# Twelve of 22 feed-forward tiles by seven products, additions on another ring, and moved clears, multiplies and a table load in the mixers

## The chip, the cores and the metric

One NeuronCore of one Trainium2 chip. The metric is the device time of one execution in microseconds, the median over several executions; lower is better. TensorE (PE in the rows) multiplies, VectorE (DVE), ScalarE (ACT) and GpSimd (POOL) work on its results, SyncE (SP) issues the transfers. Each engine takes its own instructions in order.

## What is computed

Two layers over 512 tokens of width 1024, in float32. A layer is a half-weighted feed-forward network, a mixer, and a second such network; an RMS norm stands before each, and one at the end. The first layer's mixer ("even") joins a compressed, selected and windowed attention (8 heads) with a dilated one (8 heads); the second's is a latent attention with 16 heads.

```python
for l in range(DEPTH):
    x = x + 0.5 * _swiglu(_rms_norm(x, ffn1_norm[l]), ffn1_w_gate[l], ffn1_w_up[l], ffn1_w_down[l])
    h = _rms_norm(x, mix_norm[l])
    x = x + (_even_mixer(h, ...) if l % 2 == 0 else _mla_mixer(h, ...))
    x = x + 0.5 * _swiglu(_rms_norm(x, ffn2_norm[l]), ffn2_w_gate[l], ffn2_w_up[l], ffn2_w_down[l])
return _rms_norm(x, final_norm)

def _swiglu(x, w_gate, w_up, w_down):
    return (jax.nn.silu(x @ w_gate) * (x @ w_up)) @ w_down
```

## The kernel before

x stays on the chip, transposed: eight tiles x0 to x7 of 128 features by 512 tokens. Seven stages follow one another: feed-forward f0, the even mixer, f1, f2, the latent mixer, f3, the final norm. Every product is made of three matmuls (`mm3`, L206 to L210): each operand is split in a high and a low part, and high·high, low·high and high·low are added in PSUM. A weight chunk is split when it has arrived: ScalarE copies the high part (wh, L160), VectorE subtracts for the low part (wl, L161).

**Feed-forward** (`ffn`, from L340). The hidden width 2816 is 22 tiles of 128, worked in two halves of 11. A tile is the gate and the up projection, silu of the one times the other, and a split (fah, fal). In the plain way ("nine") these are 48 matmuls of 512 columns, from two weight chunks. The tiles listed in `SEVEN` (L32) are computed by `seven` (L296): gate and up weights form a 2 by 2 block matrix, and x's features and tokens another, and seven block products (A11, S2, S1, S3, A12, S4, A22), each of 12 matmuls with 256 columns, take the place of eight; VectorE forms the weight sums S1 to S4 (s1 to s4, L174), splits seven blocks (L181) and combines the products (fv, fm, fn, fg, L325 to L334). After the 11 tiles of a half come the down products (L377 to L388): 8 blocks of 33 matmuls of 512 columns, each block evicted by a multiply into a temporary t and an addition into x[m]. The temporary is from the ring `t` (`self.tmp`, 4 buffers).

**Norm** (`norm`, `rms`, `squares`, `rstd`, `spread`, L212 to L275). x is split into xh (ScalarE, L217) and xl (VectorE, L218). ScalarE squares each x[k] into a buffer of the ring `t`, the first into `of` (L229); POOL adds six of them to `of` (L231); PE sums over the partitions (L241); POOL raises to the power −1/2 (rcol, L251); PE transposes it and ScalarE copies it out (rrow, L260, L261). The projections run with x unscaled; rrow and rcol come in at the evictions.

**Mixers.** A plan written by hand (`EVEN`, `MLA`) lists the units (projections, V, scores, outputs). In the even mixer, `cmp_probs` makes the compressed branch's probabilities: exp on ScalarE (L721), POOL's multiply with the mask (L722), VectorE's sum, POOL's multiply with the reciprocal (L729), PE's transposes (L732). `values` (L483) projects V into banks of the ring pa.

The order on each engine is set by the scheduler of the language, from a time line that it estimates; rings of buffers and banks (w, wh, wl three deep; fg and fa two; fn, fv, fm, s1 to s4 one; PSUM pa and pb two, pt three, pc one) bound how far it can run ahead.

Of the kernel before, what the change touches and what calls it, by code (L numbers as in the profile page):

```python
# [3 lines left out]
P = 128  # L4
D, SEQ, FF = 1024, 512, 2816
KT, NF, HF = D // P, FF // P, FF // P // 2
# [18 lines left out]
def raw(ap):  # L25
    return ap.bitcast(F32)
# [4 lines left out]

SEVEN = (4, 6, 8, 10, 12, 14, 16, 18, 20)  # L32

# [44 lines left out]
class Core:  # L78
# [185 lines left out]
    def rms(self, tiles, eng=None):  # L264
        col = self.rstd(self.squares(tiles, eng), D)
        return col, self.spread(col, self.keep.tile([P, SEQ], F32, name="rrow", bufs=2))

    def norm(self, gi):
        xs = [self.split(self.x[k], self.g[:, gi * 8 + k:gi * 8 + k + 1], "x", 8) for k in range(KT)]
        if gi == 0:  # L270
            with self.tc.issue_after(self.last.ins):
                col, row = self.rms(self.x, self.nc.vector)
        else:
            col, row = self.rms(self.x)
        return xs, col, row  # L275
# [64 lines left out]
    def ffn(self, name, l, gi, then=None):  # L340

        nc = self.nc
        with self.tc.tile_pool(name="ff", bufs=1, reuse_waits="tile") as sb:
# [3 lines left out]
            for half in range(2):  # L347
# [30 lines left out]
                for m in range(KT):  # L378
                    p = self.bank(("pc", "pt")[m % 2])
                    for i in range(HF):  # L380
                        if blk % 8 == 0:
                            cur = self.chunk(name + "_d", l, half, blk // 8)
                        c = slice(blk % 8 * P, blk % 8 * P + P)
                        self.mm3(p, cur[0][:, c], cur[1][:, c], ah[i], al[i], start=i == 0, stop=i == HF - 1)
                        blk += 1
                    t = self.tmp()
                    nc.vector.tensor_tensor(t, p, R, OP.mult)
                    nc.vector.scalar_tensor_tensor(self.x[m], t, 0.5, self.x[m], OP.mult, OP.add)  # L388
# [80 lines left out]
    def pt_tiles(self, sb):  # L469
        t = [sb.tile([P, 11, P], F32R, name=f"pt{c}") for c in "hl"]  # L470
        for x in t:
            self.nc.vector.memset(raw(x[:, 0, :]), 0.0)
        return t
# [8 lines left out]

    def values(self, sb, parts, xs, scale=None, more=None):  # L483

# [5 lines left out]
        for k0 in range(0, 4, m):  # L490
            bank = self.bank("pa")
            for kt in range(k0, k0 + m):
# [41 lines left out]
    def even(self, gi):  # L534
        nc, a, kp = self.nc, self.a, self.keep
        with self.tc.tile_pool(name="ev", bufs=1, reuse_waits="tile") as sb:
            xs, rc, R = self.norm(gi)
            CR = sb.tile([P, SEQ], F32, name="CR")
            SR = sb.tile([P, SEQ], F32, name="SR")
# [118 lines left out]
            def compress(i):  # L658
# [8 lines left out]
                e = sb.tile([P, 2, 32], F32, name="e", bufs=2)  # L667
                nc.vector.memset(z, 0.0)
                nc.vector.tensor_copy(z[:, :, 0:31], hid[:, :62].rearrange("p (a b) -> p a b", b=31))
# [9 lines left out]
                for g in range(2):  # L679
                    hr = sb.tile([P, 4, 32], F32, name="hr")  # L680
                    nc.vector.tensor_copy(hr, z[:, g:g + 1, :].to_broadcast([P, 4, 32]))
                    vg = vp[:, 64 * g:64 * g + 64]
                    nc.tensor.matmul(vg, hr, w2[:, 1, 0:64], start=True, stop=True)
                    vc = C["v", g] = sb.tile([P, 4, P], F32R, name=f"vc{g}")
                    nc.vector.memset(raw(vc), 0.0)
                    for j in range(4):
                        s = slice(32 * j, 32 * j + 32)
                        nc.scalar.activation(vc[s, j, 0:64], vg[s], AF.Copy)
                        nc.vector.tensor_tensor(vc[s, j, 64:128], vg[s], raw(vc[s, j, 0:64]), OP.subtract)

            def gate(kt, p):

                gt = C["g"][:, kt, :]
                nc.vector.tensor_scalar(gt, p, rc[:, kt:kt + 1], None, OP.mult)
                nc.scalar.activation(gt, gt, AF.Exp, scale=-1.0)
                nc.vector.tensor_scalar(gt, gt, 1.0, None, OP.add)
                nc.vector.reciprocal(gt, gt)

            def nsa_vals():
# [4 lines left out]
            def cmp_probs(g):  # L704
# [10 lines left out]
                def sp(x):  # L715
                    return x.rearrange("p (a b) -> p a b", b=4).unsqueeze(3).to_broadcast([P, 4, 4, 32])
# [4 lines left out]
                nc.scalar.activation(t, t, AF.Exp, scale=-1.0)  # L721
                nc.gpsimd.tensor_tensor(t, t, mcmp[:, 1].unsqueeze(2).to_broadcast([P, 4, 4, 32]), OP.mult)  # L722
                nc.vector.tensor_reduce(st[:, 1], t, AX.X, OP.add)
# [4 lines left out]
                                        C["g"][:, :, 12 * g:12 * g + 12:3], OP.mult)  # L728
                nc.gpsimd.tensor_tensor(t, t, sp(st[:, 2]), OP.mult)  # L729
                pt = self.bank("pt")  # L730
# [21 lines left out]
    def mla(self, gi):  # L752
        nc, a, kp = self.nc, self.a, self.keep
        with self.tc.tile_pool(name="ml", bufs=1, reuse_waits="tile") as sb:
            xs, rc, R = self.norm(gi)


# [57 lines left out]
            def vals(g):  # L815
                vk = slice(512 + g % 2 * 256, 768 + g % 2 * 256)
                kv = W["kv"]
                vs[g] = self.values(sb, lambda k: (kv[0][:, vk], kv[1][:, vk]), [cn[2]])

# [218 lines left out]
```

## Time and profile before

| | |
|---|---|
| median of 3 runs | 1947.82 us (1947.81 to 1949.94) |
| profiled execution, its own time | 1949.46 us |
| its span in the trace | 1947.70 us |
| mean granted clock of TensorE | 0.988 |
| f0, even mixer, f1, f2 | 0 to 365, to 667, to 1027, to 1381 us |
| latent mixer, f3, final norm | to 1575, to 1928, to 1948 us |

The profile is one execution. Its trace holds for every instruction when it started and ended, on which engine, from which line, and what released it. Busy shares are averages over the seven stages; a stretch with PE busy for its whole length is bounded there, and in the others the list of PE's waits tells who was late. The granted clock is that of TensorE, 1.00 for 2.4 GHz and 0.5 for 1.2 GHz.

### The profile page before, as it was taken

To read this page: it belongs to the slowest core of one execution; us is meant where nothing else is said; L and a number is where in the kernel's file an instruction comes from. 1 tells how busy PE (TensorE), PEld (TensorE's weight loads), DVE (VectorE), ACT (ScalarE), POOL (GpSimd) and SP (SyncE) were. 2 spreads that over 40 slices of the span, in tenths; PEclk is the share of its full clock that TensorE was granted. 3 is DMA by queue.
4 is the path that set the end of the run, shared out by engine and by line. 5 is a ranking of instruction groups with operands and counts; after the bars stand their busy time and mean duration, and the time that the engine had idled before them with its cause. 6 is when DMAs were issued, how large, how long until landed. Compare 5 with 4: busy or idle time off the path is not lost.

```text
span 1947.7 us, 26837 instructions
## 1 busy us (share of the span) xinstructions
PE 1906.6 (98%) x10418; PEld 1653.7 (85%) x10418; DVE 1276.3 (66%) x2272; ACT 875.3 (45%) x1511; POOL 272.8 (14%) x287
## 2 busy tenths in 40 slices
PE   9999999899999999999999999999899999999997
PEld 6888998778897788888888988998788878888986
DVE  8664665468888877456656664674489786646653
ACT  7432443346576654224435432442378664324421
POOL 0000000264444400000002000000256220000001
PEclk9999999899999999999999999999999999999998
DMA  4233233322111133333332332332310123333231
GB/s 172 90 109 98 87 98 108 115 81 87 55 55 34 41 100 98 98 98 97 109 98 87 98 109 87 98 119 89 122 33 23 58 83 102 104 100 96 91 107 52
DMA packets 49839, 174.59 MB, mean 90 GB/s; under 512 B 5792, under 2 KB 6048, under 8 KB 49712
## 3 DMA queue, kind: packets, MB, share of 16 engines
q1 hardware_dynamic: 48960, 171.74, 28.1%
q8 instruction: 81, 1.33, 0.3%
q10 hardware_dynamic: 720, 1.08, 0.1%
q14 instruction: 46, 0.38, 0.1%
q0 software_dynamic: 32, 0.07, 0.0%
HBM read 170.76 MB, written 2.10 MB: 89 GB/s over the span
## 4 chain that ended last, share of the span: by engine, by line
PE 71%; issue 19%; DVE 4%; ACT 3%; POOL 2%; DMA 0%; POOLq 0%; ACTq 0%; DVEq 0%
PE pa L208 8%; PE pa L209 8%; PE pa L210 8%; PE pb L209 5%; PE pb L210 5%; PE pb L208 5%; PE pt L208 5%; PE pt L209 5%; PE pt L210 5%; PE pc L210 3%; PE pc L208 3%; PE pc L209 3%; PE pc L435 2%; PE pt L424 2%; PE pb L603 1%
## 5 line engine op out<-in xcount | busy, mean ns | idle before, releaser
L161 DVE TENSOR_TENSOR wl<-w,wh 128x1024 fp32r<-128x1024 f32 x241 | 305.2, 1267 | 247.9 <-ACT wh L160 247.4
L160 ACT ACTIVATE wh<-w 128x1024 fp32r<-128x1024 f32 x241 | 254.6, 1057 | 459.9 <-PE pt L209 188.6
L208 PE MATMUL pa<-xh,wh 128*128 128x512 f32 (+1 forms) x784 | 294.4, 376 | 5.8 <-ACT wh L160 2.3
L209 PE MATMUL pa<-xl,wh 128*128 128x512 f32 (+1 forms) x784 | 292.5, 373 | 0.0
L210 PE MATMUL pa<-xh,wl 128*128 128x512 f32 (+1 forms) x784 | 292.2, 373 | 0.0
L231 POOL TENSOR_TENSOR of<-of,t 128x512 f32<-128x512 f32 x36 | 56.0, 1554 | 1375.1 <-issue 1005.6
L209 PE MATMUL pb<-xl,wh 128*128 128x512 f32 (+1 forms) x704 | 244.2, 347 | 0.2
L208 PE MATMUL pb<-xh,wh 128*128 128x512 f32 (+1 forms) x704 | 243.9, 346 | 0.1
L210 PE MATMUL pb<-xh,wl 128*128 128x512 f32 (+1 forms) x704 | 243.5, 346 | 0.0
L208 PEld LDWEIGHTS pa<-xh,wh 128*128 128x128 f32 x784 | 148.8, 190 | 33.8 <-ACT wh L160 3.7
L210 PEld LDWEIGHTS pa<-xh,wl 128*128 128x128 f32 x784 | 148.8, 190 | 26.3 <-DVE wl L161 0.8
L209 PEld LDWEIGHTS pa<-xl,wh 128*128 128x128 f32 x784 | 149.2, 190 | 24.2 <-DVE xl L218 0.2
L209 PEld LDWEIGHTS pb<-xl,wh 128*128 128x128 f32 x704 | 133.4, 189 | 18.6 <-DVE xl L218 2.6
L208 PEld LDWEIGHTS pb<-xh,wh 128*128 128x128 f32 x704 | 133.4, 189 | 16.9 <-ACT wh L160 0.5
L210 PEld LDWEIGHTS pb<-xh,wl 128*128 128x128 f32 x704 | 133.4, 189 | 16.3 <-DVE wl L161 0.4
L180 ACT ACTIVATE wh<-w 128x512 fp32r<-128x512 f32 x72 | 45.5, 632 | 210.7 <-PE pb L209 198.4
L208 PE MATMUL pc<-fah,wh 128*128 128x512 f32 x352 | 137.0, 389 | 0.0
L209 PE MATMUL pc<-fal,wh 128*128 128x512 f32 x352 | 137.0, 389 | 0.0
L210 PE MATMUL pt<-fah,wl 128*128 128x512 f32 x352 | 136.9, 389 | 0.0
L210 PE MATMUL pc<-fah,wl 128*128 128x512 f32 x352 | 136.9, 389 | 0.0
L208 PE MATMUL pt<-fah,wh 128*128 128x512 f32 x352 | 136.9, 389 | 0.0
L209 PE MATMUL pt<-fal,wh 128*128 128x512 f32 x352 | 136.9, 389 | 0.0
(255 smaller groups left out, 4115.4 us busy)
## 6 DMA issues: line engine op xcount, KB each, us to landing
w<-f_g SPq DMA_DIRECT2D x88, 512.0 KB, 3.5
w<-f_u SPq DMA_DIRECT2D x88, 512.0 KB, 3.5
w<-f_d SPq DMA_DIRECT2D x88, 512.0 KB, 3.5
w<-ev_in SPq DMA_DIRECT2D x16, 512.0 KB, 3.5
w<-ev_out SPq DMA_DIRECT2D x8, 512.0 KB, 3.3
w<-mla_out SPq DMA_DIRECT2D x8, 512.0 KB, 3.2
x<-x SPq DMA_DIRECT2D x8, 256.0 KB, 5.1
w<-ev_vb SPq DMA_DIRECT2D x4, 512.0 KB, 3.3
```

The source lines that it names most:

```text
L160: nc.scalar.activation(h[:, :cols], w[:, :cols], AF.Copy)
L161: nc.vector.tensor_tensor(l[:, :cols], w[:, :cols], raw(h[:, :cols]), OP.subtract)
L180: nc.scalar.activation(h[:, c], src, AF.Copy)
L208: nc.tensor.matmul(out, wh, xh, start=start, stop=False)
L209: nc.tensor.matmul(out, wh, xl, start=False, stop=False)
L210: nc.tensor.matmul(out, wl, xh, start=False, stop=stop)
L231: eng.tensor_tensor(parts[0], parts[0], sq, OP.add)
L424: nc.tensor.transpose(ps[:, i * P:(i + 1) * P], pt[:, c:c + P], self.ident)
L435: nc.tensor.matmul(ps[:, q0:], v(kt), PT[j][:, b, :], start=start and kt == 0 and j == 0, stop=stop and kt == 3 and j == 1)
L603: nc.tensor.matmul(ps[:, :n], q[qi][:, qt * P:(qt + 1) * P], kd[ki][j][:, :n], start=j == 0, stop=j == 1)
```

## The change

Six things. (1) `SEVEN` lists twelve tiles in place of nine, and some stand beside one another: (4,5), (7,8), (13,14), (16,17), (19,20). (2) The down phase's temporary comes from the ring `fg` of the feed-forward pool, not from `t`. (3) `warm_exp`, after the norm of both mixers, computes one exp whose result nobody reads. (4) Three clears move from VectorE to POOL. (5) The first V of the latent mixer takes its banks from pb. (6) In the compressed branch the mask comes in at the gate column (four small VectorE operations) in place of POOL's multiply with the mask, and VectorE does the multiply with the reciprocal. Line numbers after the change are 5 higher from `norm` on, then up to 8.

```diff
--- before.py
+++ after.py
@@ -29,7 +29,7 @@
-SEVEN = (4, 6, 8, 10, 12, 14, 16, 18, 20)
+SEVEN = (4, 5, 7, 8, 10, 11, 13, 14, 16, 17, 19, 20)
 FFNS = {"f0": ("f1", 0, 0), "f1": ("f2", 0, 2), "f2": ("f1", 1, 3), "f3": ("f2", 1, 5)}
@@ -264,6 +264,11 @@
     def rms(self, tiles, eng=None):
         col = self.rstd(self.squares(tiles, eng), D)
         return col, self.spread(col, self.keep.tile([P, SEQ], F32, name="rrow", bufs=2))
+
+    def warm_exp(self):
+
+        e = self.keep.tile([P, 4], F32, name="rcol", bufs=16)
+        self.nc.scalar.activation(e[:, 0:1], self.x[KT - 1][:, 0:1], AF.Exp, scale=0.0)
     def norm(self, gi):
         xs = [self.split(self.x[k], self.g[:, gi * 8 + k:gi * 8 + k + 1], "x", 8) for k in range(KT)]
@@ -383,7 +388,7 @@
                         c = slice(blk % 8 * P, blk % 8 * P + P)
                         self.mm3(p, cur[0][:, c], cur[1][:, c], ah[i], al[i], start=i == 0, stop=i == HF - 1)
                         blk += 1
-                    t = self.tmp()
+                    t = sb.tile([P, SEQ], F32, name="fg", bufs=2)
                     nc.vector.tensor_tensor(t, p, R, OP.mult)
                     nc.vector.scalar_tensor_tensor(self.x[m], t, 0.5, self.x[m], OP.mult, OP.add)
             if then is not None:
@@ -469,7 +474,7 @@
     def pt_tiles(self, sb):
         t = [sb.tile([P, 11, P], F32R, name=f"pt{c}") for c in "hl"]
         for x in t:
-            self.nc.vector.memset(raw(x[:, 0, :]), 0.0)
+            self.nc.gpsimd.memset(raw(x[:, 0, :]), 0.0)
         return t
     def project(self, xs, *key):
@@ -480,7 +485,7 @@
                      start=k == 0, stop=k == KT - 1)
         return p
-    def values(self, sb, parts, xs, scale=None, more=None):
+    def values(self, sb, parts, xs, scale=None, more=None, tag="pa"):
         nc = self.nc
@@ -488,7 +493,7 @@
         v = sb.tile([P, 4, 4, P], F32R, name="v", bufs=2)
         m = SEQ // c
         for k0 in range(0, 4, m):
-            bank = self.bank("pa")
+            bank = self.bank(tag)
             for kt in range(k0, k0 + m):
                 p = bank[:, (kt - k0) * c:(kt - k0 + 1) * c]
                 t = slice(kt * P, kt * P + P)
@@ -535,6 +540,7 @@
         nc, a, kp = self.nc, self.a, self.keep
         with self.tc.tile_pool(name="ev", bufs=1, reuse_waits="tile") as sb:
             xs, rc, R = self.norm(gi)
+            self.warm_exp()
             CR = sb.tile([P, SEQ], F32, name="CR")
             SR = sb.tile([P, SEQ], F32, name="SR")
             nc.sync.dma_start(CR, a["cos_p"])
@@ -665,7 +671,7 @@
                                          start=l0 == 0, stop=l0 == 15)
                 z = sb.tile([P, 2, 32], F32, name="z", bufs=2)
                 e = sb.tile([P, 2, 32], F32, name="e", bufs=2)
-                nc.vector.memset(z, 0.0)
+                nc.gpsimd.memset(z, 0.0)
                 nc.vector.tensor_copy(z[:, :, 0:31], hid[:, :62].rearrange("p (a b) -> p a b", b=31))
                 nc.scalar.activation(e, z, AF.Exp, scale=-1.0)
                 nc.vector.tensor_scalar(e, e, 1.0, None, OP.add)
@@ -682,7 +688,7 @@
                     vg = vp[:, 64 * g:64 * g + 64]
                     nc.tensor.matmul(vg, hr, w2[:, 1, 0:64], start=True, stop=True)
                     vc = C["v", g] = sb.tile([P, 4, P], F32R, name=f"vc{g}")
-                    nc.vector.memset(raw(vc), 0.0)
+                    nc.gpsimd.memset(raw(vc), 0.0)
                     for j in range(4):
                         s = slice(32 * j, 32 * j + 32)
                         nc.scalar.activation(vc[s, j, 0:64], vg[s], AF.Copy)
@@ -695,6 +701,8 @@
                 nc.scalar.activation(gt, gt, AF.Exp, scale=-1.0)
                 nc.vector.tensor_scalar(gt, gt, 1.0, None, OP.add)
                 nc.vector.reciprocal(gt, gt)
+
+                nc.vector.tensor_scalar(gt[:, 0::3], gt[:, 0::3], mcmp[:, 1, kt, 0:1], None, OP.mult)
             def nsa_vals():
                 c = [self.chunk("ev_vsw", i) for i in range(3)]
@@ -719,14 +727,13 @@
                 nc.vector.tensor_reduce(st[:, 0], t, AX.X, OP.min)
                 nc.vector.tensor_tensor(t, t, sp(st[:, 0]), OP.subtract)
                 nc.scalar.activation(t, t, AF.Exp, scale=-1.0)
-                nc.gpsimd.tensor_tensor(t, t, mcmp[:, 1].unsqueeze(2).to_broadcast([P, 4, 4, 32]), OP.mult)
                 nc.vector.tensor_reduce(st[:, 1], t, AX.X, OP.add)
                 nc.vector.tensor_scalar(st[:, 1], st[:, 1], 1.0, None, OP.max)
                 nc.vector.reciprocal(st[:, 2], st[:, 1])
                 nc.vector.tensor_tensor(st[:, 2].rearrange("p (a b) -> p a b", b=4),
                                         st[:, 2].rearrange("p (a b) -> p a b", b=4),
                                         C["g"][:, :, 12 * g:12 * g + 12:3], OP.mult)
-                nc.gpsimd.tensor_tensor(t, t, sp(st[:, 2]), OP.mult)
+                nc.vector.tensor_tensor(t, t, sp(st[:, 2]), OP.mult)
                 pt = self.bank("pt")
                 for qt in range(4):
                     nc.tensor.transpose(pt[:, qt * P:(qt + 1) * P], t[:, qt].rearrange("p a b -> p (a b)"),
@@ -753,6 +760,7 @@
         nc, a, kp = self.nc, self.a, self.keep
         with self.tc.tile_pool(name="ml", bufs=1, reuse_waits="tile") as sb:
             xs, rc, R = self.norm(gi)
+            self.warm_exp()
             CQ = [sb.tile([P, SEQ], F32, name=f"CQ{i}") for i in range(2)]
@@ -815,7 +823,7 @@
             def vals(g):
                 vk = slice(512 + g % 2 * 256, 768 + g % 2 * 256)
                 kv = W["kv"]
-                vs[g] = self.values(sb, lambda k: (kv[0][:, vk], kv[1][:, vk]), [cn[2]])
+                vs[g] = self.values(sb, lambda k: (kv[0][:, vk], kv[1][:, vk]), [cn[2]], tag="pb" if g == 0 else "pa")
             def keys(hp):
                 p = self.bank("pa")
```

VectorE in f0's second half, the pair of tiles 13 and 14. After the change; w_1934 and w_1935 are tile 14's weights, wl_1945 its first low parts (A11 and S2), wl_1952 those of S1 and S3; fm_2014, fn_2012 and fg_2011 are tile 13's combinations.

```order
L174 TENSOR_TENSOR s4_1941<-w_1934,s2_1939 128x512
L181 TENSOR_TENSOR wl_1945<-w_1934,wh_1944 128x512
L181 TENSOR_TENSOR wl_1945<-s2_1939,wh_1944 128x512
L330 TENSOR_TENSOR fv_2013<-fm_2014,pa_2008 128x256
L181 TENSOR_TENSOR wl_1952<-s1_1938,wh_1951 128x512
L333 TENSOR_TENSOR fm_2014<-fv_2013,pt_2010 128x512
L181 TENSOR_TENSOR wl_1952<-s3_1940,wh_1951 128x512
L335 TENSOR_TENSOR fn_2012<-fm_2014,pt_2010 128x256
L338 TENSOR_TENSOR fg_2011<-fm_2014,pb_2009 128x512
L181 TENSOR_TENSOR wl_1959<-w_1934,wh_1958 128x512
L181 TENSOR_TENSOR wl_1959<-s4_1941,wh_1958 128x512
L339 TENSOR_TENSOR fg_2011<-fg_2011,rrow_179 128x512
```

Tile 14's splits stand between tile 13's combinations, the first of them ahead of all of these; before, tile 13 was a nine.

ScalarE at the end of f0's down phase, before: wh are splits of weight chunks, xh the split of x for the even mixer, t the squares of the next norm.

```order
L217 ACTIVATE xh_3181<-x6_71,g_63 128x512
L160 ACTIVATE wh_3122<-w_3120 128x1024
L160 ACTIVATE wh_3258<-w_3256 128x1024
L229 ACTIVATE t_3191<-x1_66 128x512
L229 ACTIVATE t_3194<-x2_67 128x512
L229 ACTIVATE t_3197<-x3_68 128x512
L229 ACTIVATE t_3200<-x4_69 128x512
L217 ACTIVATE xh_3185<-x7_72,g_63 128x512
L229 ACTIVATE t_3203<-x5_70 128x512
L229 ACTIVATE t_3206<-x6_71 128x512
L229 ACTIVATE t_3209<-x7_72 128x512
```

The same place after the change:

```order
L229 ACTIVATE t_3410<-x5_70 128x512
L160 ACTIVATE wh_3295<-w_3293 128x1024
L217 ACTIVATE xh_3388<-x6_71,g_63 128x512
L229 ACTIVATE t_3413<-x6_71 128x512
L160 ACTIVATE wh_3329<-w_3327 128x1024
L160 ACTIVATE wh_3467<-w_3465 128x1024
L217 ACTIVATE xh_3392<-x7_72,g_63 128x512
L229 ACTIVATE t_3416<-x7_72 128x512
L271 ACT_TABLE_LOAD
L271 ACTIVATE rcol_3438<-x7_72 128x1
```

The squares of x5 and x6 have moved between the splits; one square and the load of the table (L271) stand behind the last chunk.

POOL at the start of the even mixer, before:

```order
L231 TENSOR_TENSOR of_3189<-of_3189,t_3206 128x512
L251 TENSOR_TENSOR rcol_3220<-rv_3221,mhalf_62 128x4
L552 TENSOR_TENSOR CR_3231<-CR_3231,rrow_3224 128x512
L553 TENSOR_TENSOR SR_3232<-SR_3232,rrow_3224 128x512
L566 TENSOR_TENSOR t_3407<-t_3407,SR_3232 128x512
```

The same place after the change:

```order
L231 TENSOR_TENSOR of_3396<-of_3396,t_3413 128x512
L477 MEMSET pth_3461 128x128
L477 MEMSET ptl_3462 128x128
L674 MEMSET z_3934 128x64
L674 MEMSET z_4295 128x64
L691 MEMSET vc0_4307 128x512
L691 MEMSET vc1_4320 128x512
L251 TENSOR_TENSOR rcol_3427<-rv_3428,mhalf_62 128x4
L558 TENSOR_TENSOR CR_3440<-CR_3440,rrow_3431 128x512
```

Six clears have come between the last addition of squares and the power (L251).

## Rows read from the trace of the kernel before

**Rows 1.** Page, part 1: busy us (share of span) x instructions, whole kernel.
```profile
PE 1906.6 (98%) x10418; PEld 1653.7 (85%) x10418; DVE 1276.3 (66%) x2272; ACT 875.3 (45%) x1511; POOL 272.8 (14%) x287
```

**Rows 2.** By stretch: window, us, PE, PEld, DVE, ACT, POOL busy (x), PEclk, DMA, GB/s.
```profile
200.08:221.06 20.98, 20.98 (x134) 19.09 (x132) 15.05 (x24) 8.92 (x14) 0.00 (x0) 1.00 0.29 101
129.33:189.20 59.87, 59.87 (x267) 49.55 (x265) 27.96 (x34) 12.43 (x14) 0.00 (x0) 1.00 0.35 105
364.82:409.75 44.93, 39.43 (x213) 34.65 (x212) 20.59 (x30) 14.17 (x21) 26.75 (x18) 0.89 0.29 95
1381.17:1423.42 42.25, 37.12 (x178) 31.35 (x176) 21.60 (x36) 19.68 (x31) 14.52 (x11) 0.88 0.27 92
1927.61:1947.70 20.09, 9.13 (x49) 8.43 (x47) 4.93 (x9) 4.72 (x8) 4.81 (x4) 0.61 0.27 104
```

**Rows 3.** PE's waits: tile and line, releaser, total us, count, longest.
```profile
PE pa L208 <- DVE x L531: 5.4, 5, 3.1
PE pa L498 <- ACT t L229: 5.0, 1, 5.0
PE pt L887 <- POOL of L231: 4.5, 1, 4.5
PE pa L499 <- DVE xl L218: 2.1, 1, 2.1
PE pt L260 <- POOL rcol L251: 1.8, 1, 1.8
PE pa L208 <- DVE v L512: 1.7, 1, 1.7
PE pt L732 <- POOL t L729: 1.3, 1, 1.3
```

**Rows 4.** PE in order of time: start us, duration us, line, operation, out<-in, form.
```profile
200.08 0.28 PE L208 MATMUL pa<-xh,wh 128*128 128x256 f32 x1
210.15 0.40 PE L208 MATMUL pa<-xh,wh 128*128 128x512 f32 x1
221.06 0.28 PE L208 MATMUL pa<-xh,wh 128*128 128x256 f32 x1
```

**Rows 5.** VectorE in order of time, a seven tile of f0, same columns.
```profile
238.00 1.29 DVE L181 TENSOR_TENSOR wl<-s,wh 128x512 fp32r<-128x512 f32 x2
...
249.04 1.22 DVE L161 TENSOR_TENSOR wl<-w,wh 128x1024 fp32r<-128x1024 f32 x1
250.18 0.68 DVE L328 TENSOR_TENSOR fm<-fv,pt 128x512 f32<-128x512 f32 x1
250.90 0.42 DVE L330 TENSOR_TENSOR fn<-fm,pt 128x256 f32<-128x256 f32 x1
251.23 0.68 DVE L333 TENSOR_TENSOR fg<-fm,pb 128x512 f32<-128x512 f32 x1
```

**Rows 6.** In order of time, start of the even mixer: ScalarE, POOL, VectorE, ScalarE.
```profile
365.80 1.66 ACT L229 ACTIVATE t<-x 128x512 f32<-128x512 f32 x3
...
366.49 9.59 POOL L231 TENSOR_TENSOR of<-of,t 128x512 f32<-128x512 f32 x6 [340.04 <-ACT t L229]
...
368.27 2.31 DVE L161 TENSOR_TENSOR wl<-w,wh 128x1024 fp32r<-128x1024 f32 x1
...
423.81 1.28 ACT L410 ACT_TABLE_LOAD   x1
```

**Rows 7.** VectorE in order of time, compressed branch, first group.
```profile
500.24 2.85 DVE L580 SCALAR_TENSOR_TENSOR q<-t,q 64x512 fp32r<-64x512 f32 x2
...
505.26 0.63 DVE L531 TENSOR_TENSOR x<-pa,x 128x512 f32<-128x512 f32 x1
```

**Rows 8.** VectorE in order of time, start of the latent mixer.
```profile
1410.18 0.69 DVE L773 SCALAR_TENSOR_TENSOR cnl<-t,cnh 128x512 fp32r<-128x512 f32 x1 [0.70 <-ACT cnh L772]
```

**Rows 9.** In order of time, final norm: ScalarE, POOL.
```profile
1929.26 2.19 ACT L229 ACTIVATE t<-x 128x512 f32<-128x512 f32 x4 [6.85 <-DVE x L388]
...
1938.42 1.02 POOL L902 TENSOR_TENSOR rcol<-rv,mhalf 128x4 f32<-128x4 f32 x1 [4.45 <-DVE rv L901]
```

## The prediction

> **What bounds the kernel now.** I first read the shares of busy time: PE 98%, DVE 66%, ACT 45%, POOL 14% [rows 1]. A number near 100% over six different stages says little about one stage, so the second view is the table by stretch [rows 2]. Its first two lines are the inside of a feed-forward stage: PE is busy for the whole of 20.98 us at a granted clock of 1.00, while DVE works 15.05 us, ACT 8.92; in a down phase PE is busy for 59.87 of 59.87 us, DVE for 27.96. There only fewer or shorter matmuls shorten the time. The other three lines are the start of the even mixer, the start of the latent mixer and the final norm: PE is busy for 39.43 of 44.93, 37.12 of 42.25 and 9.13 of 20.09 us, at clocks of 0.89, 0.88 and 0.61. There PE waits, and the list of its waits says for whom [rows 3]: 4.5 us for POOL's additions of squares before the final norm; 5.0 us for a ScalarE square (t, L229) before the latent mixer's first V; 1.8 + 1.7 + 2.1 us in the start of the even mixer; up to 3.1 us at once for VectorE's L531, and 1.3 us for POOL's L729, in the mixer's compressed branch. Each of these ends has a queue behind it, so each is followed on the engine named.
>
> A time of this kernel can tell a change from none at about 0.2%, 3.9 us. The sum goes against the profiled execution (1949.46 us); the median of the runs is 1.64 us lower, which I take off at the end.
>
> **The change, part by part.**
>
> *Twelve more tiles by seven products* (three more in each of four stages). Two neighbouring tiles start 200.08 to 210.15 (seven products) and 210.15 to 221.06 (nine) [rows 4]: 10.07 and 10.91 us. That agrees with 84 matmuls of 256 columns at .120 and 48 of 512 at .227. Twelve times 0.84 is **−10.1**, if PE stays the bound. The Trainium skill's page "TensorE: Matmul & The Clock Gate", section "Wait — 56ns, not 53.3ns?", gives columns over 2.4 GHz plus about 2.5 ns; this would be 109 and 216 ns, 9.2 and 10.4 us a tile, and −14.3 as an estimate. The rows show both shapes some 10 and 5% above that, so the sum stays with −10.1.
>
> Does PE stay the bound? VectorE does far more for a seven: sixteen operations of 512 columns at .60 from start to start, and three of 256 columns at .33 (250.90 to 251.23) [rows 5], 10.6 us, against 4.1 for a nine (two of 1.14, three of .60). Before, every seven stood next to a nine: 14.7 of 20.98 us (the row has 15.05). Now there are five pairs of sevens in each stage: 21.2 us of VectorE against 20.1 of PE. Alone that would not hold, but each pair has a nine before and behind it: three tiles need 25.3 of VectorE and 31.05 of PE. What decides is whether VectorE can run ahead. From the start of the pair's first tile, PE wants the second tile's four block groups at 10.07, 12.95, 15.8 and 18.7 us; their buffers come free at 2.88, 5.76, 8.64 and 10.07 (24 matmuls a pair of blocks). The least slack is 7.2 us, with two splits and up to four weight sums at .60 in it, 3.6. The changed order has the second tile's splits ahead of the first tile's tail, as the fence of VectorE's rows shows. I cost the pairs at nothing; what covers them is that slack.
>
> *The additions' temporary from the gate ring.* It adds and removes no instruction; it frees the ring t for the squares, and the six additions of each next norm move into the down phase. Four stages gain, each by its own chain:
> - Start of the even mixer. Before, three squares at .55 each run in a row at 365.80 after the last product, and six POOL additions take 9.59 us from 366.49 [rows 6]; the sums, the column's power and the row follow. After, only x7's square is left. PE's own work in the stretch is 96 matmuls of 256 columns and 96 of 512, 33.3 us; to it come 1.4 for sums and transposes, .7 for x7's low part and .5 for the first weight split: 35.9 against 44.93, **−9.0** (−6 to −10: the rcol wait of 1.8 may stay, since six clears now stand before the power on POOL).
> - Start of the latent mixer, where V also changes its bank. Before, the V products wait 5.0 us for pa to be released by work that stands behind the squares, though their operand was ready at 1410.18 + .69 [rows 8]; the clock then is lower for about 4 us. After: 96 matmuls of 512, 21.8, and 2.5 around them, then a chain from the last projection to the first scores. It has six VectorE steps of .60 and one of 1.14 with 1 us of waits, five ScalarE copies at .55, and .85 for the first products: 9.3. PE has only 6.4 of work in it, so about 2.9 of waiting stays, with some 1.2 lost to the clock. 34.8 against 42.25: **−7.5** (−5 to −9).
> - Final norm. Four squares in a row begin at 1929.26, POOL adds behind them, and the power of the column begins only at 1938.42 [rows 9]. With six additions done during the products, x7's square (.55) and the sum's matmuls are left after the last product's eviction (1.2 for two VectorE steps), so that the power can begin near 1931.3: **−7.0** (−6 to −7.4).
> - f1 to f2 has no wait of this kind in the list: 0.
>
> What speaks against it: the first split beside POOL's additions took 2.31 us (368.27) [rows 6], the same form alone 1.22 [rows 5], so each of the 24 additions that move can cost VectorE 1.09 us. The skill's page "SBUF — State Buffer", section "Who interferes with whom", has that rule: a VectorE instruction with two SBUF inputs contends with a GpSimd one that reads SBUF. The trace agrees by these two rows. In the down phase VectorE is idle for 31.9 of 59.87 us [rows 2], which covers it; I cost it at nothing, and the loss of that cover is a rival below.
>
> *Exp table early.* The load of 1.28 us stood on ScalarE at 423.81 before the first softmax [rows 6]; it moves under the products: **−1.3** (0 to −2.7, with the clock).
>
> *The compressed branch.* POOL's mask multiply goes, and its other multiply moves to VectorE. The wait of 3.1 us was for VectorE's L531, which began at 505.26, after two slow q operations (2.85 us for two) [rows 7] and a split. Before, the transposes' wait and the lower clock behind it cost 3.1 + 1.5; after, they wait for one VectorE multiply, about 1 us, with .4 for the clock: **−3.2** (0 to −4.6). The second group's wait for POOL's L729, 1.3: **−1.5** with the clock (0 to −2.4). The four small operations on the gate columns run when the gates are made, before any of this: 0, and 2.4 us at most at .60 each.
>
> *Clears to POOL.* On VectorE they lay beside products, 0; on POOL, ahead of the power, they may keep the 1.8 us wait, which is in the even start's bound.
>
> Sum: 10.1 + 9.0 + 7.5 + 7.0 + 1.3 + 3.2 + 1.5 = 39.6. From 1949.46 that is 1909.9, and 1.64 lower at the median: **1908 us**. All the ends together give 1902 and 1921 (46.2 and 27.1 removed); both at once are unlikely, and the forecast's own range is 1901 to 1915.
>
> **Rivals.**
> - *The mixers give half back.* A removed wait shows the next late thing. Of the 29.5 us outside the tiles 14.8 come back: 1947.8 − 10.1 − 14.8 = 1923. For it: the chains in the mixers pass through three engines, and the even start has three different releasers [rows 3]. Against it: two of the ends (even start, final norm) are bounded by PE's own matmuls. 0.20.
> - *Pairs bound by VectorE.* 21.2 − 20.14 = 1.06 for each of 20 pairs, 21.2: 1929. For it: VectorE's longer sum. Against it: 5.8 us of spare time in three tiles. 0.05.
> - *Squares slow the down phase's splits.* 24 × 1.09 = 26.2 on PE's path: 1934. For it: the 2.31 us row. Against it: 31.9 us of idle VectorE in 59.87. 0.03.
> - *Slower: the second seven of a pair waits at the first one's end.* fn, fg, fa, fal and A22's low part have single or double buffers; if the second tile's first split stood behind them, PE would wait for 2.1 us of VectorE, one ScalarE copy (.55) and one more split (.60): 3.3 us in each of 20 pairs, 66 us: 1974. It decides from (39.6 + 3.9) / 20 = 2.2 us a pair on. For it: VectorE's queue is in order and an operation waiting for PE's last product blocks what follows. Against it: the changed order puts splits ahead. 0.03.
> - *No effect.* The squares could still be placed after the last block. The changed order of ScalarE shows them among the blocks. 0.01.
>
> **How the numbers follow.** Forecast 0.68. The range 1899 to 1924 takes in its bounds and the first rival, 0.88 in all less the forecast's own misses. Faster by over 0.2%: all but the last two, 0.95; the same 0.02, for no effect and mixtures; slower 0.03.
>
> **What would show it.** A stretch of seven, seven, nine in f0's second half should last 31.05 us with PE busy throughout; a stall in it, with VectorE or ScalarE as releaser before a product of A11 or S2, makes the pair rivals true. The even start should last about 36 us, the latent one 35, the final norm 13, with POOL's additions spread over the down phases. The 5.0 and 4.5 us waits should be gone. If the stretches outside the feed-forward stages shorten by under 20 us, the first rival holds; a down phase above 60 us would show the additions in VectorE's way.

## The result, and the profile after

The changed kernel takes 1913.88 us (median of 4 runs, 1913.83 to 1914.83), the kernel before 1948.68 (4 runs, 1947.81 to 1949.94): 0.9822 of it, with a 95% interval of 0.9805 to 0.9839. The forecast was 1908, with a range of 1899 to 1924. The profiled execution took 1913.86 us, its span is 1911.7.

The page's shares, to be held against [rows 1]:

```profile
PE 1883.0 (98%) x10850; PEld 1657.4 (87%) x10850; DVE 1354.5 (71%) x2438; ACT 903.4 (47%) x1585; POOL 274.6 (14%) x291
```

PE is busy for 23.6 us less, the span is 36.0 us shorter; VectorE rose from 66% to 71%. The table by stretch, whose columns are those of [rows 2]: three tiles (13, 14 and 15: seven, seven, nine) of f0's second half, f0's second down phase, the start of the even mixer, the start of the latent mixer, the final norm.

```profile
209.32:240.38 31.06, 31.06 (x217) 29.17 (x216) 25.98 (x43) 14.54 (x24) 0.00 (x0) 1.00 0.34 102
302.50:362.34 59.84, 59.84 (x265) 49.57 (x264) 29.88 (x34) 20.48 (x26) 8.82 (x6) 1.00 0.30 92
362.34:397.84 35.50, 35.50 (x213) 31.73 (x212) 17.73 (x24) 12.47 (x17) 19.07 (x18) 1.00 0.40 129
1362.13:1396.93 34.80, 33.23 (x179) 28.11 (x177) 18.97 (x32) 17.71 (x27) 6.43 (x7) 1.00 0.35 121
1898.46:1911.72 13.26, 5.35 (x49) 5.11 (x47) 4.79 (x9) 3.05 (x5) 1.02 (x1) 0.80 0.41 158
```

The three tiles last 31.06 us with PE busy throughout (31.05 forecast). Six POOL additions (8.82 us) now lie inside the down phase, which lasts 59.84 us as before. The even start takes 35.50 in place of 44.93 us, without a wait and at full clock; the latent one, to its first scores, 34.80 in place of 42.37 (the window of [rows 2] ends just ahead of these); the final norm 13.26 in place of 20.09. POOL in order of time shows it: additions between the down phase's blocks, the clears (1.4 us in all) right after the last product, and the power at 369.74, which waits for none of them.

```profile
321.12 1.86 POOL L231 TENSOR_TENSOR of<-of,t 128x512 f32<-128x512 f32 x1 [294.70 <-ACT t L229]
328.99 1.29 POOL L231 TENSOR_TENSOR of<-of,t 128x512 f32<-128x512 f32 x1 [6.02 <-ACT t L229]
...
357.90 1.29 POOL L231 TENSOR_TENSOR of<-of,t 128x512 f32<-128x512 f32 x1 [5.50 <-ACT t L229]
362.57 0.21 POOL L477 MEMSET pth<- 128x128 f32 x1 [3.37 <-PE pt L210]
...
363.02 0.99 POOL L691 MEMSET vc<- 128x512 f32 x2
369.74 1.02 POOL L251 TENSOR_TENSOR rcol<-rv,mhalf 128x4 f32<-128x4 f32 x1 [5.73 <-DVE rv L246]
```

Of PE's waits in [rows 3] those for L229, L231, L251 and L512 are gone. The largest left within the mixers are these:

```profile
PE pb L609 <- DVE mn L412: 3.8, 4, 2.3
PE pb L209 <- DVE kl L837: 2.4, 1, 2.4
PE pb L208 <- ACT kh L836: 1.5, 1, 1.5
PE pt L739 <- DVE t L736: 1.4, 1, 1.4
```

The time by stage, from PE's first matmul of each stage in the two traces ("rest" reaches to the first matmul behind the next stage's norm; before, that is 24 and 17 us past the ends of the mixers at 667 and 1575):

| stretch | before | after | difference | forecast |
|---|---|---|---|---|
| f0, f1, f2, f3 | 1390.80 | 1380.98 | −9.8 | −10.1 |
| even start | 44.93 | 35.50 | −9.4 | −9.0 |
| even rest | 281.27 | 279.04 | −2.2 | −6.0 |
| latent start | 42.37 | 34.80 | −7.6 | −7.5 |
| latent rest | 168.24 | 168.16 | −0.1 | 0 |
| final norm | 20.09 | 13.26 | −6.8 | −7.0 |

### The profile page after: what moved, and what is told of

Its sections match the earlier page's. It is cut to its first block, busy times and chain, and to the rows that moved or that the text cites. A ratio compares the mean times of both kernels' runs of the same rounds, so it can differ in the third digit from the quotient of the medians.

```text
span 1911.7 us, 27981 instructions
## 1 busy us (share of the span) xinstructions
PE 1883.0 (98%) x10850; PEld 1657.4 (87%) x10850; DVE 1354.5 (71%) x2438; ACT 903.4 (47%) x1585; POOL 274.6 (14%) x291
## 5 line engine op out<-in xcount | busy, mean ns | idle before, releaser
L160 ACT ACTIVATE wh<-w 128x1024 fp32r<-128x1024 f32 (+1 forms) x217 | 229.2, 1057 | 357.7 <-PE pt L209 98.3
L161 DVE TENSOR_TENSOR wl<-w,wh 128x1024 fp32r<-128x1024 f32 (+1 forms) x217 | 273.0, 1259 | 159.4 <-ACT wh L160 158.3
L208 PE MATMUL pa<-xh,wh 128*128 128x512 f32 (+1 forms) x736 | 269.1, 366 | 2.8 <-ACT wh L160 2.2
L210 PE MATMUL pa<-xh,wl 128*128 128x512 f32 (+1 forms) x736 | 268.2, 364 | 0.5 <-DVE wl L161 0.5
L209 PE MATMUL pa<-xl,wh 128*128 128x512 f32 (+1 forms) x736 | 268.7, 365 | 0.0
L231 POOL TENSOR_TENSOR of<-of,t 128x512 f32<-128x512 f32 x36 | 55.9, 1552 | 1319.6 <-issue 892.5
L209 PE MATMUL pb<-xl,wh 128*128 128x256 f32 (+1 forms) x704 | 233.9, 332 | 0.2
L208 PE MATMUL pb<-xh,wh 128*128 128x256 f32 (+1 forms) x704 | 233.6, 332 | 0.0
L210 PE MATMUL pb<-xh,wl 128*128 128x256 f32 (+1 forms) x704 | 233.3, 331 | 0.0
L180 ACT ACTIVATE wh<-w 128x512 fp32r<-128x512 f32 x96 | 60.7, 632 | 237.9 <-PE pb L209 159.2
L180 ACT ACTIVATE wh<-s 128x512 fp32r<-128x512 f32 x192 | 114.9, 622 | 55.9 <-PE pa L209 26.3
```

The lines of the kernel that those rows point to most:

```text
L160: nc.scalar.activation(h[:, :cols], w[:, :cols], AF.Copy)
L161: nc.vector.tensor_tensor(l[:, :cols], w[:, :cols], raw(h[:, :cols]), OP.subtract)
L180: nc.scalar.activation(h[:, c], src, AF.Copy)
L208: nc.tensor.matmul(out, wh, xh, start=start, stop=False)
L209: nc.tensor.matmul(out, wh, xl, start=False, stop=False)
L210: nc.tensor.matmul(out, wl, xh, start=False, stop=stop)
```

## The experiments

**One part undone each.** First the ring:

```diff
-                    t = sb.tile([P, SEQ], F32, name="fg", bufs=2)
+                    t = self.tmp()
```

> The changed kernel with the down phase's temporary back in the ring t; all else as changed. Theory (the ring carries the gain of all three edges): the even start goes from 35.5 us back to about 44, the final norm from 13.3 to about 20, the latent start loses 3 to 8 us; in all 19 to 24 us more than the changed kernel, about 1935. Rival (the bank, the clears and the table load carried the two mixer starts, the ring only the final norm): 7 us more, about 1921. The feed-forward tiles stay at 20.15 us a pair in both.

1935.12 us, 21 us more. The same three stretches by window (to the first scores in the latent one; the even start here reaches 403.90):

```profile
362.37:403.90 41.53, 38.26 (x213) 33.52 (x212) 17.07 (x24) 15.55 (x23) 27.92 (x24) 0.92 0.31 101
1368.33:1412.19 43.86, 37.88 (x178) 31.73 (x177) 22.01 (x35) 21.82 (x33) 15.40 (x13) 0.89 0.27 88
1912.88:1933.00 20.12, 9.13 (x49) 8.43 (x47) 4.92 (x9) 4.72 (x8) 4.82 (x4) 0.62 0.27 104
```

The latent start is at 43.86, the final norm at 20.12, both back; the even start is at 41.5, 6.0 of its 9.4 us back, with the waits for the power (1.8) and for the first eviction of V (1.5). So the ring carries the latent start and the final norm whole, and of the even start two thirds, where the theory expected about 44 us. The first V takes its banks from pb in this run too, and the latent start is long all the same: the bank alone would not have shortened it.

Of the other 3.4 us of the even start 2.1 is the wait for xl (L218) in [rows 3], which did not come back. The traces show what took it away. Before, the six clears stood on VectorE between the last product's multiply and the addition to x7, ahead of xl:

```profile
365.02 0.69 DVE L387 TENSOR_TENSOR t<-pt,rrow 128x512 f32<-128x512 f32 x1 [3.10 <-PE pt L210]
365.68 0.17 DVE L472 MEMSET pth<- 128x128 f32 x1
...
366.19 1.02 DVE L685 MEMSET vc<- 128x512 f32 x2
367.13 1.21 DVE L388 SCALAR_TENSOR_TENSOR x<-t,x 128x512 f32<-128x512 f32 x1
...
370.50 1.75 DVE L218 SCALAR_TENSOR_TENSOR xl<-x,g,xh 128x512 fp32r<-128x512 f32 x1
```

In the run with the ring undone they are on POOL, and xl begins 3.3 us after the last product in place of 5.7:

```profile
365.67 1.16 DVE L218 SCALAR_TENSOR_TENSOR xl<-x,g,xh 128x512 fp32r<-128x512 f32 x1 [0.55 <-ACT xh L217]
```

1.4 of these 2.4 us are the clears; the rest is instructions that took longer before. No run moved the clears alone, but the new list alone (the last run below) leaves the wait at 2.1.

The bank of V, and the clears, in two runs (of the clears the first of three lines, all changed alike):

```diff
-                vs[g] = self.values(sb, lambda k: (kv[0][:, vk], kv[1][:, vk]), [cn[2]], tag="pb" if g == 0 else "pa")
+                vs[g] = self.values(sb, lambda k: (kv[0][:, vk], kv[1][:, vk]), [cn[2]], tag="pa")
...
-            self.nc.gpsimd.memset(raw(x[:, 0, :]), 0.0)
+            self.nc.vector.memset(raw(x[:, 0, :]), 0.0)
```

> The changed kernel with the latent mixer's first V back in banks of pa. Theory (what held pa were the squares behind the last products, and these now run in the down phase): 0 to 1 us more, 1914 to 1915, no wait of a V product for pa above 1 us. Rival (the bank itself was the cause): the wait of 5.0 us comes back, about 1919.

> The changed kernel with the clears back on VectorE. Theory (they lie beside products on either engine): the even start stays at 41.2 us to its first scores, the total within 1 us of 1913.9, and what differs comes from the order in the mixers. Rival (POOL's six clears ahead of the power are a cost that the forecast's bounds held, or the clears on VectorE were one): the even start moves by 1 us or more.

1913.58 and 1913.39 us. With the additions on their new ring neither part is worth a time that these runs can tell: V's wait of 5.0 us did not come back with pa (one of 1.2 us is there; the latent start is 0.7 us longer, its rest 1.1 shorter), and the even start to its first scores is 41.21 us with the clears on either engine.

The compressed branch:

```diff
-                nc.vector.tensor_scalar(gt[:, 0::3], gt[:, 0::3], mcmp[:, 1, kt, 0:1], None, OP.mult)
...
+                nc.gpsimd.tensor_tensor(t, t, mcmp[:, 1].unsqueeze(2).to_broadcast([P, 4, 4, 32]), OP.mult)
...
-                nc.vector.tensor_tensor(t, t, sp(st[:, 2]), OP.mult)
+                nc.gpsimd.tensor_tensor(t, t, sp(st[:, 2]), OP.mult)
```

> The changed kernel with the compressed branch as before: both multiplies on POOL, no mask in the gate column. Theory (as the traces of the two kernels read: only the first group gained, the second got new waits of the same size on ScalarE's and VectorE's queues): 2 to 3.5 us more, about 1916.7, with a wait of some 3 us back in the first group and the second group's losses within 0.7 us of the changed kernel's. The forecast's terms would make it 4.7 us more, 1918.6. Rival (neither group gained from this part, the order moved for other reasons): 0.

1919.38 us, 5.5 more, above both figures. 2.5 us of it lie in the even mixer's rest, within the theory's 2 to 3.5, but partly by luck. Between places up to which both kernels have done the same matmuls, the first group takes 2.8 us more, with its wait of 3.1 back. The second takes 1.1 us less, though its waits sum to 4.7 us in both, so its losses are not within 0.7 us of the changed kernel's. Another 0.4 is gained where the gates are made, and 1.2 is lost behind the wait for the second scores, which is as long as in the changed kernel: the matmuls behind it stay longer at the lower clock. What the edit itself costs there is 1.3 us. PE's waits:

```profile
PE pa L208 <- DVE x L536: 5.6, 4, 3.1
PE pt L738 <- POOL t L735: 1.3, 1, 1.3
PE pt L429 <- DVE cl L743: 0.7, 1, 0.7
```

The 0.4 is the small operation on the gate column. In the changed kernel one of the four stands on VectorE ahead of the minimum over a score tile (L412), for which PE's next scores wait, as the trace shows:

```profile
435.51 0.23 DVE L705 TENSOR_SCALAR gt<-gt,mcmp 128x8 f32<-128x8 f32 x1
435.65 0.24 DVE L700 TENSOR_SCALAR gt<-pa,rcol 128x24 f32<-128x24 f32 x1
435.80 0.28 DVE L412 CUSTOM_DVE_ANT_0 p<-pb,mdil 128x128 f32<-128x128 f32 x1
```

The other 3.1 us lie in the latent mixer (171.25 against 168.16), where nothing was edited: the scheduler, whose time line had moved, wrote another order of instructions there. That was in neither expectation, and a total alone would have charged it to this part.

The early exp, taken out of both mixers:

```diff
-            self.warm_exp()
```

> The changed kernel without warm_exp in either mixer. Theory (in the even mixer the load of 1.28 us hid a wait for POOL's rotation and VectorE's split, so taking it away gave 0.6; in the latent mixer the load has room): 0.6 to 1.2 us more, about 1914.8. The forecast's term: 1.3 more from the even mixer alone. Rival (both mixers wait for the load at the lower clock): 2.6 and more, above 1916.5.

> The changed kernel without warm_exp again, now timed more than once. Theory (0.6 us of the 2.7 us that it cost is the load in the even mixer's chain, and 0.4 in the latent mixer; the other 1.7 was a stretch at the lower clock near 600 us that falls in some executions and not in others): the fastest executions lie at 1914.5 to 1915, some at 1916.5. Rival (the lower clock there belongs to the missing early load): all executions at 1916.3 or more.

1916.62 in the first run; 1916.81, 1916.38, 1916.58 and 1914.97 later: 2.6 us more at the median. The order on PE, VectorE and POOL in the even mixer is that of the changed kernel. Of the wait before the second scores 0.6 us came back (2.93 against 2.30). Most of the rest lies 180 us later, in 10 us in which PE gets 38 matmuls done at a mean clock of 0.83 here, and 48 at 1.00 in the changed kernel; first this kernel (the run of four), then the changed one:

```profile
593.00:603.00 10.00, 7.46 (x38) 6.17 (x37) 8.11 (x17) 5.70 (x12) 0.45 (x1) 0.83 0.20 61
```

```profile
592.00:602.00 10.00, 7.46 (x48) 6.14 (x47) 9.42 (x23) 6.89 (x16) 1.00 (x2) 1.00 0.20 55
```

So the early load is worth 0.6 us at its place. Both profiled executions without it show the lower clock there, and one of the four times (1914.97) lies where 0.6 and 0.4 us alone would put it, which the rival did not allow; that this execution had no such stretch is inferred from its time. But the rival is not done with: the changed kernel and the five other profiled runs here that keep its order in the even mixer, but for the clears (the bank, the clears, fifteen tiles twice, sixteen) all have the early load, and all show 1.00 at that place. Whether the missing load brings the lower clock there, in most executions and not in all, stays open; the order and the waits ahead of that place are the same but for the 0.6 us.

**The second group.** In the changed kernel the wait for POOL's L729 is gone, but the group's waits rose from 3.7 to 4.7 us, at three other places (PE, VectorE, POOL and ScalarE, each in order of time; the first VectorE row is the first group's):

```profile
588.07 0.50 PE L208 MATMUL pa<-oh,wh 128*128 128x512 f32 x1 [1.09 <-DVE st L731]
595.32 0.51 PE L440 MATMUL pc<-pth,v 128*128 128x512 f32 x1 [1.11 <-ACT pth L432]
597.09 0.44 PE L429 MATMUL pt<-ident,p 128*128 128x128 f32 x2 [1.26 <-DVE cl L744]
```

```profile
491.41 0.69 DVE L736 TENSOR_TENSOR t<-t,st 128x512 f32<-128x512 f32 x1
...
586.09 0.69 DVE L730 TENSOR_REDUCE st<-t 128x16 f32<-128x512 f32 x1 [0.70 <-ACT t L729]
586.69 0.68 DVE L570 TENSOR_TENSOR t<-pa,CR 128x512 f32<-128x512 f32 x1
...
587.98 1.22 DVE L161 TENSOR_TENSOR wl<-w,wh 128x1024 fp32r<-128x1024 f32 x1
589.11 0.68 DVE L536 TENSOR_TENSOR x<-pa,x 128x512 f32<-128x512 f32 x1
...
590.62 1.68 DVE L736 TENSOR_TENSOR t<-t,st 128x512 f32<-128x512 f32 x1
```

```profile
590.42 1.33 POOL L573 TENSOR_TENSOR t<-t 128x512 f32<-128x512 f32 x1
```

```profile
591.78 1.29 ACT L585 ACTIVATE q<-t 64x512 fp32r<-64x512 f32 x2 [4.78 <-POOL t L573]
593.10 1.06 ACT L160 ACTIVATE wh<-w 128x1024 fp32r<-128x1024 f32 x1
594.18 0.60 ACT L743 ACTIVATE ch<-pt 128x512 fp32r<-128x512 f32 x1
594.67 1.08 ACT L432 ACTIVATE pth<-pt 128x512 fp32r<-128x512 f32 x2
```

VectorE waits for the exp at 586.09 with the reduction at the head of its queue, and a projection's rotation, a weight split and L536, which releases an output bank, stand behind it: PE waits 1.09. The multiply that was moved from POOL takes 1.68 us beside POOL's part of the rotation (L573); the first group's, with nothing on POOL, takes 0.69. The rule of the Trainium skill's page "SBUF — State Buffer", section "Who interferes with whom", that a VectorE instruction with two SBUF inputs contends with a GpSimd one that reads SBUF, agrees with these rows. The transposes then come without a wait, but their copy (L743) stands behind two copies of q and a weight split on ScalarE. A run moved that projection:

```diff
-     [... "o2 p1 q11 o3", "", ...
+     [... "o2 p1 o3", "q11", ...
```

> The changed kernel with one unit of the even mixer's plan (the projection q11) moved from beside the second group's probabilities (p1) to the next place in the list. Theory (the second group gained nothing because q11's two ScalarE copies, its weight split and its VectorE steps stand ahead of the group's copies of the transposes): the two waits of 1.3 and 1.5 us behind the transposes near 595 us shrink to under 1 us together, 1.5 to 2.5 us less, about 1912. Rival (the chain of the second group itself, from scores to transposes, ends last): nothing there changes, within 0.5 us of 1913.9.

1923.36 us, 9.5 more. At its place the theory was right in part: the wait at 588 is gone and those behind the transposes are 0.7 and 0.6, 1.3 together and not under 1, which gains 1.3 us there and not 1.5 to 2.5:

```profile
594.69 0.49 PE L440 MATMUL pc<-pth,v 128*128 128x512 f32 x1 [0.71 <-ACT pth L432]
595.81 0.44 PE L429 MATMUL pt<-ident,p 128*128 128x128 f32 x2 [0.63 <-DVE cl L744]
...
654.31 0.73 PE L208 MATMUL pa<-oh,wh 128*128 128x512 f32 x2 [2.06 <-ACT oh L622]
655.66 0.54 PE L209 MATMUL pa<-ol,wh 128*128 128x512 f32 x1 [0.62 <-POOL ol L623]
```

But the outputs at the mixer's end waited 2.1 and 0.6 for oh and ol, presumably because the projection, now late, held back the heads that use it; the even rest as a whole took 5.0 us more, and the latent mixer got another order again (172.56 against 168.16). What is gained at its place is lost again behind it.

**How many tiles by seven products.**

```diff
-SEVEN = (4, 5, 7, 8, 10, 11, 13, 14, 16, 17, 19, 20)
+SEVEN = (4, 5, 6, 8, 9, 10, 11, 12, 14, 15, 16, 18, 19, 20, 21)
```

> The changed kernel with fifteen of 22 tiles by seven products: (4,5,6), (8 to 12 across the halves), (14,15,16), (18 to 21). Theory (TensorE stays the bound, as in the pairs at 20.15 us; three sevens and a nine want 35.9 us of VectorE and 41.1 of TensorE): 12 more tiles at 0.83, 10 us less, about 1904, with runs of sevens at 10.07 us a tile. Rival (VectorE's longer work shows once three sevens follow one another): stalls within the runs, 0.5 to 3 us in each of 16, 1912 or more.

1909.88 us. The feed-forward stages gave 9.9 us, with three sevens in 30.23 us and no stall; the even rest took 1.3 us more, the latent rest 4.9. The order in the even mixer is that of the changed kernel on every engine, and so are the waits: its 1.3 us are the clock behind the wait for the second scores, where PE gets 18 matmuls done in 6 us at a mean clock of 0.57, and 22 at 0.72 in the changed kernel.

> The changed kernel with all tiles from 4 to 21 by seven products, 18 of 22. Theory: TensorE saves 24 x 0.83 = 20 us, but VectorE needs 10.6 us for each seven against 10.07; a run of eleven falls 5.8 us behind, a run of seven 3.7, against some 3.6 us by which it can run ahead, so stalls of 0 to 3 us at the end of each half: 1896 to 1904. Rival (TensorE stays the bound throughout, since VectorE begins each half far ahead): 1894. Rival (VectorE cannot run ahead in long runs, the queue's order blocks it): 0.5 us and more for each tile, 1910 or more.

1906.17 us, with tiles 4 to 21, above the theory's 1904. Six more tiles in each stage save some 1.5 us and not 5: VectorE is busy 109.5 of 115.4 us in the second half, PE waits for weight splits within the run and the down phases begin among the last products of the seven. That loses some 3.5 us a stage, of which 1.9 show as waits in f0.

```profile
187.39:302.83 115.44, 114.20 (x925) 112.63 (x924) 109.49 (x192) 58.49 (x104) 0.00 (x0) 1.00 0.32 106
```

```profile
263.07 0.38 PE L208 MATMUL pa<-xh,wh 128*128 128x256 f32 x1 [0.41 <-ACT wh L180]
```

Here VectorE is the bound, and a run of eleven reaches past what it can run ahead, as the theory had it, though the loss is larger. In the same run the second group's waits are smaller by themselves (3.6 us in place of 4.7, and 1.3 us of time), and there the scheduler put L536 and the split ahead of the waiting reduction. The run with the ring undone has that order too, and the same gain. With V back in pa, the latent mixer's order is the same whatever the list of tiles, so two more runs took that:

> The changed kernel with the fifteen tiles of the run before by seven products, and the latent mixer's first V back in banks of pa. Theory (the fifteen tiles gave their 9.9 us in the feed-forward stages; the 6.2 us that the run lost came from another order of instructions in the latent mixer, which the scheduler made, and from the clock; with V in pa the order there is that of the run with the bank undone): that run's 1913.6 less 9.9, about 1903.7, with the latent mixer's rest at 167.0 us. Rival (the loss in the mixers belongs to the longer runs of sevens, whatever the order): 1909 or more.

> As the fifteen tiles with V in pa, and one more tile by seven products (4 to 6, 8 to 15, 17 to 21). Theory (TensorE stays the bound while a nine stands within eight sevens; the stalls of the run with eighteen came from eleven in a row): 0.83 less in each of four stages, 3.3 us less than with fifteen, about 1900.4. Rival (VectorE falls behind in a run of eight that crosses the down phase, or of five at the end): 0.5 to 3 us of stalls in each stage, 1902 to 1912.

1905.43 us (1904.42 to 1907.25) and 1904.04 (1903.78 to 1904.78); of the kernel before, 0.9778 (0.9764 to 0.9793) and 0.9771 (0.9756 to 0.9785). The latent rest was 166.6 and 166.8: the loss of the run with fifteen there belonged to the order. The 1.3 us of the even rest stayed in both. The sixteenth tile gave 0.15 in f1, f2 and f3 in place of 0.83, as the rival had it: its run of five at the end lets the down phase begin among the run's last products, and there PE waits for VectorE's eviction (L392, in fg), which is half of what is missing:

```profile
314.65 0.50 PE L208 MATMUL pc<-fah,wh 128*128 128x512 f32 x1 [0.33 <-DVE fg L392]
```

Both beat the changed kernel, the one with sixteen by 9.8 us at the medians.

Last, the new list alone in the kernel before:

> The kernel before with the new list of twelve tiles alone. Theory (0.83 us for each of 12 tiles, the pairs run without a stall, the order in the mixers is that of the kernel before): 9.9 us less than the kernel before, about 1938 to 1939.6 by which of its own times one takes, pairs at 20.15 us. Rival (the pairs hold only because the additions' temporary left the ring t): stalls in the pairs or before the down phases, 1943 or more.

1943.82 us in one run, above the theory's 1939.6 and at the rival's bound. But its reason fails: pairs take 20.15 us, and the stages f1 to f3 save what they should (0.82 and 1.62 a half). The order in the mixers is that of the kernel before. What is missing is the program's start (f0 saves 1.1 in place of 2.5; the clock of its first 20 us is 0.83, 0.91 in the changed kernel), 0.8 in the even rest and 2.0 in the latent start, whose granted clock is 0.84 in place of [rows 2]'s 0.88 with the same order and the same wait of 5 us. 1.5 of these 2.0 lie ahead of that wait: seven matmuls from 1390.4 on take 0.43 us each in place of 0.23, after no wait of PE above 0.2 us in that stage. Why the clock falls there the traces do not say. The kernel before itself lay between 1947.8 and 1952.5 in these studies, the changed one between 1913.8 and 1914.8: spells at the lower clock that fall in some executions and not in others would make such a spread; these profiles suggest it, no run tested it.

## Why the prediction was right, and where it was off

The direction, the size and the range held, and the mechanism at all three edges. By its own steps:

- *Twelve more tiles* (−10.1): −9.8, pairs at 20.15, no stall. The rivals of the pairs, the slower one too, did not occur. The figure of the Trainium skill's page "TensorE: Matmul & The Clock Gate", section "Wait — 56ns, not 53.3ns?", would have made it −14.3 as an estimate; the trace does not agree, and its .120 and .227 decided. Where VectorE becomes the bound showed with eighteen tiles.
- *The ring*: the three edges gave −9.4, −7.6 and −6.8 against −9.0, −7.5 and −7.0. The run without it gave back 21 us: the latent start and the final norm whole, 6.0 of the even start, where the moved clears have a part. That the latent start met its 34.8 us so closely is in part luck: PE waited 1.6 us of it and not 2.9, and lost nothing to the clock where 1.2 was allowed, but was busy for 33.2, where the terms (21.8, 2.5 and 6.4) make 30.7. And behind the wait of 5.0 us before the change the clock was lower for some 8 us, not 4 (0.50 from 1412.2 to 1416.5, 0.59 on to 1421).
- *Additions beside the down phase's splits*: 59.84 us with six additions within. The contention shown by [rows 5, 6] costs VectorE time that it has; the rival did not occur.
- *Exp table early* (−1.3): 0.6 at its place. The step took the load for the end of the chain; behind it POOL's rotation and VectorE's split were nearly as late. After the change ScalarE's copy of q waits 0.40 us for POOL:

```profile
413.48 1.28 ACT L585 ACTIVATE q<-t 64x512 fp32r<-64x512 f32 x2 [0.40 <-POOL t L573]
```

- *The compressed branch*: the first group −2.5 against −3.2. The four operations on the gate columns were priced at 0 and cost 0.4. The second group (−1.5) is where the forecast failed: +0.5, with 1.0 more of waits, while the kernel before lost time there to the clock (0.66 from 597 to 602 us). It priced the one wait that [rows 3] names and did not follow what was late next on VectorE's and ScalarE's queues, so the first rival, a new late thing for a removed wait, held at this one place. With the exp's 0.6 these make the even rest's −2.2. Outside the tiles 26.2 of the 29.5 us came.
- *Clears and bank*: 0 each in the changed kernel, as the clears were priced. But the reading behind that price, that the clears lay beside products on VectorE, fails for the six before the even mixer: they stood ahead of xl, and with the squares at the edge PE waited 2.1 us for it. The bank had been told together with the ring, and has no part in its gain.
- *The median 1.64 us under the profiled execution*: this was taken off, and nothing like it came. The runs of before lay at 1947.8 and at 1949.5 to 1949.9, the profiled one among the latter; the changed kernel's profiled run is its median. With 3.6 us from the sum, 1.6 from here and 0.4 between span and time, these make the 5.7 us from 1908.2 to 1913.9.

## What to carry to other kernels

Where a stage's edge waits for a row of small operations, look at which ring of buffers holds them there: one name changed moved 18 additions off three edges and gave three fifths of the gain. A removed wait is worth its length only up to the next operation in the queues of the other engines, so walk those queues before pricing it. And where a scheduler writes the order, compare stage by stage, not totals: an edit here moved stages that it did not touch by up to 5 us, and a variant whose order there stays the same is worth choosing for that alone.

## What had not been expected of the hardware

The granted clock behind a wait differs between executions and between kernels with the same order and the same waits (0.83 and 1.00 over the same 10 us of the program near 594 us), so that an early table load came out at 2.6 us, of which 0.6 lie at its place; whether the rest belongs to the load is open. The clock also fell where PE had not waited above 0.2 us in that stage (0.50 from 1390.3 to 1393.4 us with the new list alone, 1.00 at the same place of the kernel before). And the executions of the kernel before, with 5 us waits at its edges, spread over 4.7 us, those of the changed one over 1; but these are thirteen in four studies against four in one, and four of the kernel with fifteen tiles spread over 2.8.
